# Weight k-tiles 1088 bytes apart instead of 1024, and the mixed activations at a multiple of 64 bytes

## The chip, the core and the metric

The program runs on one core of one Trainium2 chip. The metric is the device time of one execution in microseconds (us); shorter is better. The engines are TensorE (PE in the rows; PEld is its loading of weights), VectorE (DVE), ScalarE (ACT), GpSimd (POOL) and SyncE (SP, which here only issues transfers). SBUF is the on-chip memory of 128 partitions, PSUM the memory into which TensorE accumulates. All byte counts below are counts within one partition.

## The reference

One decoder block on 256 tokens of width 2048, all in float32:

```python
h = rms_norm(x, norm_mix_w)
proj = h @ w_in                       # q, k, v, z, xbc, dt, gate_a, gate_s
attn = sliding_window_attention(q, k, v, sinks, bias) @ w_attn_out
ssm = mamba2_mixer(z, xbc, dt, ...) @ w_ssm_out
mixed = sigmoid(gate_a) * attn + sigmoid(gate_s) * ssm
x = x + mixed @ w_out
u = causal_depthwise_conv(rms_norm(x, norm_ffn_w) @ w_ffn_up)
g, up = split(u, 2)
x = x + (gelu(g) * up) @ w_ffn_down
x = x + sigmoid(rms_norm(x, ple_norm_w) @ w_ple_gate) * (p @ w_ple_proj)
```

Every weight matrix is used once, so the work is a row of large products of 256 tokens with weights that come from HBM.

## The kernel before

Activations are kept with channels on partitions. A matrix of 2048 channels by 256 tokens is held as 16 k-tiles of 128 channels. To keep float32 accuracy with float32r matmuls, each activation and each weight is split in two parts, high and low: the high part is a ScalarE copy that rounds to float32r, the low part is VectorE's difference from the original. The split activations stand in tiles of `[128, k-tiles, 512]`: in each k-tile 256 columns of high parts and 256 of low parts, 2048 bytes. These tiles are `XS` (the input, for `w_in`), `YS` (for `w_ssm_out`), `AS` (for `w_attn_out`), `MS` (the mixed activations, for `w_out`), `XG` (for `w_ffn_up`, and again for `w_ple_gate`) and `FS` (for `w_ffn_down`).

Weights come in chunks of four k-tiles by 256 columns, 512 KB each. `load_chunk` (L66 to L78) issues one transfer on SP's queue into `raw` (five buffers), one ScalarE activation (L76) into `wh` and one VectorE subtraction (L77) into `wl` (three buffers each). `panel` (L95) walks over the chunks of 256 output columns and calls `products` for each k-tile:

```python
for ps, cs in zip(ps2, tiles):        # two halves of 128 output columns
    TE.matmul(ps, lhsT=wh[:, cs], rhs=x, ...)              # L84: 512 columns
for ps, cs in zip(ps2, tiles):
    TE.matmul(ps[:, 0:T], lhsT=wl[:, cs], rhs=x[:, 0:T], ...)  # L86: 256 columns
```

So one k-tile of a panel is four matmuls, called a step below: two of L84 that stream 512 columns and two of L86 that stream 256, each with a load of 128x128 weights of its own. The weights are the stationary operand, the activations the moving one. In `by_token` (L507 to L509, for q, k and v) the roles are exchanged: the stationary operand is a piece of `XS`, and the moving one a k-tile of `wh` or `wl`, 256 columns. `products_joined` (L92) is used for the very last panel.

The order of the instructions on each engine is set when the program is built. Most tiles are placed from the low end of SBUF upwards, in the order of their pools: constants, the weights' pool `wp`, small tiles, then `XS`, `YS` and the others; `MS`, `GA`, `T1` and `xt` are placed from the high end downwards.

In the built program the tiles lie as follows. Each buffer of `wh` and `wl` takes 4096 bytes and begins at a multiple of 4096, so every k-tile of weights begins at a multiple of 1024. `XS`, `YS`, `AS` and `XG` begin 64 bytes past a multiple of 2048. `FS` begins at 1472 past a multiple of 2048, which is 448 past a multiple of 512. `MS` begins at 163808, which is 480 past a multiple of 512 and 32 past a multiple of 64.

Of the kernel before, what the change touches and what calls it, by code (L numbers as in the profile page):

```python
# [10 lines left out]
F32 = mybir.dt.float32  # L11
F32R = mybir.dt.float32r
AF = mybir.ActivationFunctionType
ALU = mybir.AluOpType
# [3 lines left out]
P = 128  # L18
T = 256
D_MODEL = 2048  # L20
ND = D_MODEL // P
# [12 lines left out]
EPS = 1e-6  # L34
KC = 4
PW = 256
NEG = -1e30
RLEN = 384

# [4 lines left out]
def hybrid_block(ctx: ExitStack, tc: tile.TileContext, a: dict, out: bass.AP):  # L44
    nc = tc.nc
    V, S, G, TE = nc.vector, nc.scalar, nc.gpsimd, nc.tensor

    const = ctx.enter_context(tc.tile_pool(name="const", bufs=1))
    wp = ctx.enter_context(tc.tile_pool(name="wp", bufs=3))
# [5 lines left out]
    def acc():  # L55
        return acc_pool.tile([P, 512], F32, name="acc")

    def misc():
        return ms_pool.tile([P, 512], F32, name="ms")
# [5 lines left out]

    def load_chunk(src, kc=KC, width=PW, parts=1, before=None):  # L66
        raw = wp.tile([P, kc, width], F32, name="raw", bufs=5)
        wh = wp.tile([P, kc, width], F32R, name="wh")
        wl = wp.tile([P, kc, width], F32R, name="wl")
        n = kc // parts  # L70
        for i in range(parts):
            ks = slice(i * n, (i + 1) * n)
            if before:
                before(i)
            nc.sync.dma_start(raw[:, ks, :], src[:, ks, :])
            S.activation(wh[:, ks, :], raw[:, ks, :], AF.Copy)  # L76
            V.tensor_tensor(wl[:, ks, :], raw[:, ks, :], wh[:, ks, :].bitcast(F32), ALU.subtract)  # L77
        return wh, wl  # L78
# [32 lines left out]
    def summed(ps, name="sum", bufs=4, pool=ev):  # L111
        lo = ev.tile([P, T], F32, name="lo", bufs=4)
        S.activation(lo, ps[:, T:2 * T], AF.Copy)
        t = pool.tile([P, T], F32, name=name, bufs=bufs)
        V.tensor_tensor(t, ps[:, 0:T], lo, ALU.add)  # L115
        return t
# [10 lines left out]
    def bc(ap, shape):  # L127
        return ap.broadcast_to(shape)
# [5 lines left out]
    XS = hs_pool.tile([P, ND, 2 * T], F32R, name="XS")  # L134
# [67 lines left out]
    with tc.tile_pool(name="ssm", bufs=2) as sp:  # L202
# [28 lines left out]
        H = SSM_HEADS  # L231
# [13 lines left out]
        def step_sizes():  # L245
            raw = wp.tile([P, ND, H], F32, name="raw", bufs=5)
            nc.sync.dma_start(raw, a["w_dt"])
            psw = acc()
            for i in range(2):
                w2 = wp.tile([P, 8, 2 * H], F32R, name="wh")  # L250
                ks = slice(8 * i, 8 * i + 8)
                S.activation(w2[:, :, 0:H], raw[:, ks, :], AF.Copy)
                V.tensor_tensor(w2[:, :, H:], raw[:, ks, :], w2[:, :, 0:H].bitcast(F32), ALU.subtract)
                for k in range(8):
                    kk = 8 * i + k
                    TE.matmul(psw, lhsT=w2[:, k, :], rhs=XS[:, kk, :], start=(kk == 0), stop=(kk == ND - 1))
            scr = wp.tile([P, 8 * P], F32, name="raw", bufs=5)
            d = scr[:, 0:4 * P]
            S.activation(d, psw, AF.Copy)
            psd = misc()  # L260
            for b in range(2):
                for i in range(2):
                    TE.matmul(psd[:, b * H:(b + 1) * H], lhsT=d[:, i * T + b * P:i * T + (b + 1) * P], rhs=fold,
                              start=(i == 0), stop=(i == 1))
            dtb = scr[:, 4 * P:4 * P + H]
            nc.sync.dma_start(dtb, a["dt_bias"].partition_broadcast(P))
            ea = scr[:, 4 * P + H:5 * P]
            nc.sync.dma_start(ea, a["A_log"].partition_broadcast(P))
            S.activation(ea, ea, AF.Exp)
            xr = scr[:, 5 * P:6 * P].rearrange("p (b h) -> p b h", b=2)  # L270
            for b in range(2):
                V.scalar_tensor_tensor(xr[:, b, :], psd[:, b * H:(b + 1) * H], r_tok[:, b:b + 1], dtb,
                                       ALU.mult, ALU.add)

            e = scr[:, 6 * P:7 * P].rearrange("p (b h) -> p b h", b=2)
            V.scalar_tensor_tensor(e, xr, -1.0, xr, ALU.mult, ALU.min)
            S.activation(e, e, AF.Exp)
            z = scr[:, 7 * P:8 * P].rearrange("p (b h) -> p b h", b=2)
            V.tensor_scalar(z, e, 2.0, None, ALU.add)
            V.reciprocal(z, z)  # L280
            V.tensor_tensor(z, z, e, ALU.mult)
            z2 = scr[:, 0:P].rearrange("p (b h) -> p b h", b=2)
            V.tensor_tensor(z2, z, z, ALU.mult)
            q = scr[:, 1 * P:2 * P].rearrange("p (b h) -> p b h", b=2)
            V.tensor_scalar(q, z2, 1.0 / 17, None, ALU.mult)
            for n in (15, 13, 11, 9, 7, 5, 3):
                V.scalar_tensor_tensor(q, q, 1.0 / n, z2, ALU.add, ALU.mult)
            V.scalar_tensor_tensor(q, q, 1.0, z, ALU.add, ALU.mult)
            V.tensor_scalar(q, q, 2.0, None, ALU.mult)
            V.scalar_tensor_tensor(dt, xr, 0.0, q, ALU.max, ALU.add)  # L290
            V.scalar_tensor_tensor(dta, dt, -1.0, bc(ea.unsqueeze(1), [P, 2, H]), ALU.mult, ALU.mult)
            psa = misc()
            for c in range(2):
                TE.matmul(psa[:, c * H:(c + 1) * H], lhsT=tri, rhs=dta[:, c, :], start=True, stop=True)
            S.activation(acs, psa[:, 0:2 * H].rearrange("p (c h) -> p c h", c=2), AF.Copy)
            pah = misc()
            for c in range(2):
                TE.matmul(pah[0:H, c * P:(c + 1) * P], lhsT=dta[:, c, :], rhs=tri, start=True, stop=True)
            ach = sp.tile([H, 2 * P], F32, name="ach", bufs=1)
            S.activation(ach, pah[0:H, 0:2 * P], AF.Copy)  # L300
            nc.scalar.dma_start(acd, ach)
            pst = misc()
            TE.matmul(pst[:, 0:H], lhsT=sl32, rhs=dta[:, 0, :], start=True, stop=True)
            S.activation(dtd, pst[:, 0:H], AF.Exp)
            V.tensor_tensor(dtd, dtd, dt[:, 0, :], ALU.mult)
# [13 lines left out]
        for g in range(GROUPS):  # L319
# [60 lines left out]
            for c in range(2):  # L380
                for h in range(8):
                    j, r = h // 2, h % 2
                    TE.matmul(pys[c][r * HD:(r + 1) * HD, j * P:(j + 1) * P],  # L383
                              lhsT=xdt[:, c, h * HD:(h + 1) * HD], rhs=Es[c][:, h, :], start=True, stop=True)
# [15 lines left out]
            for pn in range(2):  # L400
                ps2 = panel(W, base, ND, XS)
                base += CH
                for i in range(2):
                    t = summed(ps2[i])
# [24 lines left out]
    for pn in range(8):  # L429
        ps2 = panel(W, base, ND, XS)  # L430
        base += CH
        for i in range(2):
            t = scaled(ps2[i], r_bc)
            S.activation(T1[:, 2 * pn + i, :], t, AF.Sigmoid)
    for pn in range(8):
        ps2 = panel(a["w_ssm_out"], pn * 2 * CH, 2 * ND, YS)
        for i in range(2):
            c = 2 * pn + i
            t = summed(ps2[i])
# [8 lines left out]
    with tc.tile_pool(name="att", bufs=2) as ap:  # L448


        tab = ap.tile([N_BUCKETS + 1, N_HEADS], F32, name="tab", bufs=1)
        V.memset(tab[N_BUCKETS:N_BUCKETS + 1, :], NEG)
        nc.sync.dma_start(tab[0:N_BUCKETS, :], a["rel_bias_table"])
# [23 lines left out]
        def normed(ps2):  # L477

            qm = ap.tile([P, 2, 4], F32, name="qm")
            for b in range(2):  # L480
                sq = ap.tile([P, 256], F32, name="ksq")
                S.activation(sq, ps2[b][:, 0:PW], AF.Square, scale=HD ** -0.5)
                V.tensor_reduce(qm[:, b, :], sq.rearrange("p (h d) -> p h d", h=4), AX.X, ALU.add)
# [3 lines left out]
            r = ap.tile([P, 2, 4], F32, name="qr")  # L487
            qn = ap.tile([P, 2, PW], F32, name="qn", bufs=3)
            for b in range(2):
                V.tensor_scalar(r[:, b, :], p[:, b, :], r_tok[:, b:b + 1], HD ** -0.5, ALU.mult, ALU.mult)  # L490
                V.tensor_tensor(qn[:, b, :].rearrange("p (h d) -> p h d", h=4),
                                ps2[b][:, 0:PW].rearrange("p (h d) -> p h d", h=4),
                                bc(r[:, b, :].unsqueeze(2), [P, 4, HD]), ALU.mult)
            return qn

        def by_token(between=None):
# [3 lines left out]
            for j in range(CH):  # L500
                wh, wl = load_chunk(W[base + j])
                for b in range(2):
                    for k in range(KC):
                        kk = j * KC + k
                        hi = XS[:, kk, b * P:(b + 1) * P]
                        lo = XS[:, kk, T + b * P:T + (b + 1) * P]
                        TE.matmul(ps2[b][:, 0:PW], lhsT=hi, rhs=wh[:, k, :], start=(kk == 0), stop=False)  # L507
                        TE.matmul(ps2[b][:, 0:PW], lhsT=hi, rhs=wl[:, k, :], start=False, stop=False)  # L508
                        TE.matmul(ps2[b][:, 0:PW], lhsT=lo, rhs=wh[:, k, :], start=False, stop=(kk == ND - 1))  # L509
# [25 lines left out]
        for g in range(N_KV):  # L535
            pk = misc()
            for b in range(2):
                for d in range(2):
                    TE.matmul(pk[d * HD:(d + 1) * HD, (1 - b) * P:(2 - b) * P],
                              lhsT=kt[:, b, g * HD:(g + 1) * HD], rhs=flip, start=True, stop=True)  # L540
# [88 lines left out]
        for kind, pn in ATT_ORDER:  # L629
# [6 lines left out]
            for i in range(2):  # L636
                t = summed(ps2[i])
# [3 lines left out]


    ms_pool2 = tc.alloc_tile_pool(name="mp2", bufs=1, side="right")
    MS = ms_pool2.tile([P, ND, 2 * T], F32R, name="MS")
    for pn in range(8):
        ps2 = panel(a["w_attn_out"], pn * CH, ND, AS)
        if pn % 4 == 0:
# [1 line left out]
        for i in range(2):  # L649
            c = 2 * pn + i  # L650
            t = summed(ps2[i])
            V.tensor_tensor(t, t, GA[:, c, :], ALU.mult)
            V.tensor_tensor(t, t, T1[:, c, :], ALU.add)
            split(MS[:, c, :], t)
    at_pool.release()
# [26 lines left out]

    residual(a["w_out"], ND, MS, g_ffn, sqa)
    ms_pool2.release()
# [33 lines left out]
    with tc.tile_pool(name="ple", bufs=2) as pp:  # L718
# [13 lines left out]
        for pn in range(8):  # L732
# [5 lines left out]
            for i in range(2):  # L738
                c = 2 * pn + i
                if pn == 7:  # L740
                    t = ev.tile([P, T], F32, name="sum", bufs=4)
                    V.tensor_tensor(t, ps2[i][:, 0:T], r3_bc, ALU.mult)
                else:
                    t = scaled(ps2[i], r3_bc)
# [107 lines left out]
```

## Time and profile before

| | |
|---|---|
| median of 3 runs | 2090.68 us (2089.81 to 2093.47) |
| profiled execution, its own time | 2089.55 us |
| its span, first to last instruction | 2087.7 us |
| mean granted TensorE clock | 0.993 |
| TensorE busy | 2046.4 us (98%) |
| VectorE busy | 1502.7 us (72%) |
| ScalarE busy | 1149.1 us (55%) |

1.9 us of the profiled execution lie outside its span. Busy times of matmuls are modelled and overlap, since matmuls are pipelined: how fast TensorE goes is read from the distance between the starts of matmuls, not from the duration of one. [...]

### The profile page before, as it was taken

What the parts mean: (1) busy time and instruction counts of PE and PEld (TensorE: products, weight loads), DVE (VectorE), ACT (ScalarE), POOL (GpSimd) and SP (SyncE); (2) the same over time, 40 slices, a digit from 0 to 9 for tenths busy, and PEclk for the clock granted to TensorE, in tenths of its full rate; (3) what the DMA queues carried; (4) which work ended last, traced back from release to release, by engine and by line L of the source; (5) the groups of instructions that cost most, each with busy time, mean ns of one, the idle gap of its engine ahead of it and who ended that gap; (6) DMA issues with size and microseconds to landing.
All of it is one profiled execution on the core that took longest, in us unless ns stands there. A gap on an engine that the chain in (4) does not pass through costs nothing.

```text
span 2087.7 us, 32510 instructions
## 1 busy us (share of the span) xinstructions
PE 2046.4 (98%) x12452; PEld 1801.5 (86%) x12452; DVE 1502.7 (72%) x2510; ACT 1149.1 (55%) x1757; POOL 181.5 (9%) x114
## 2 busy tenths in 40 slices
PE   7999999999999999999989999999999999999999
PEld 6788888888888889999868888888888888888888
DVE  7888988988755445777767667777777776555476
ACT  4667666666544444565665555555555555444454
POOL 3402222202000000101000010000000000000000
PEclk8999999999999999999999999999999999999999
DMA  5555555554455555545525655555555555555564
GB/s 191 202 183 193 181 181 178 185 183 172 172 192 192 192 192 198 181 164 170 172 95 189 230 187 191 192 192 192 191 190 189 192 189 191 192 192 188 179 208 146
DMA packets 113159, 385.49 MB, mean 185 GB/s; under 512 B 13931, under 2 KB 20972, under 8 KB 111852
## 3 DMA queue, kind: packets, MB, share of 16 engines
q1 hardware_dynamic: 103916, 366.00, 50.9%
q10 hardware_dynamic: 9088, 17.43, 2.5%
q8 instruction: 97, 1.59, 0.3%
q14 instruction: 58, 0.48, 0.1%
HBM read 381.16 MB, written 2.21 MB: 184 GB/s over the span
## 4 chain that ended last, share of the span: by engine, by line
PE 91%; DVE 4%; issue 2%; ACT 1%; POOL 1%; DMA 1%; SPq 0%; DVEq 0%; ACTq 0%; POOLq 0%
PE acc L84 53%; PE acc L86 27%; DVE wl L77 3%; PE acc L508 2%; PE acc L507 2%; PE acc L509 2%; PE ms L616 1%; PE ms L383 1%; PE acc L92 1%; ACT wh L76 0%; PE ms L607 0%; POOL zg L410 0%; POOL zg L409 0%; ACT L226 0%; PE ms L84 0%
## 5 line engine op out<-in xcount | busy, mean ns | idle before, releaser
L77 DVE TENSOR_TENSOR wl<-raw,wh 128x1024 fp32r<-128x1024 f32 (+1 forms) x700 | 888.7, 1273 | 517.9 <-ACT wh L76 515.0
L76 ACT ACTIVATE wh<-raw 128x1024 fp32r<-128x1024 f32 (+1 forms) x700 | 733.4, 1050 | 806.5 <-PE acc L84 482.9
L84 PE MATMUL acc<-XS,wh 128*128 128x512 f32 x1792 | 570.8, 398 | 9.6 <-ACT wh L76 9.5
L84 PE MATMUL acc<-XG,wh 128*128 128x512 f32 x1632 | 506.6, 392 | 0.0
L86 PEld LDWEIGHTS acc<-XS,wl 128*128 128x128 f32 x1792 | 338.0, 190 | 93.2 <-DVE wl L77 20.7
L86 PE MATMUL acc<-XS,wl 128*128 128x256 f32 x1792 | 363.3, 283 | 12.1 <-DVE wl L77 12.0
L86 PEld LDWEIGHTS acc<-XG,wl 128*128 128x128 f32 x1632 | 306.4, 188 | 67.4
L86 PE MATMUL acc<-XG,wl 128*128 128x256 f32 x1632 | 322.7, 279 | 0.0
L84 PEld LDWEIGHTS acc<-XS,wh 128*128 128x128 f32 x1792 | 276.5, 190 | 13.6 <-ACT wh L76 11.0
L84 PEld LDWEIGHTS acc<-XG,wh 128*128 128x128 f32 x1632 | 247.2, 188 | 0.0
L84 PE MATMUL acc<-FS,wh 128*128 128x512 f32 x704 | 219.6, 393 | 0.0
L84 PE MATMUL acc<-YS,wh 128*128 128x512 f32 x512 | 159.0, 392 | 0.0
L86 PEld LDWEIGHTS acc<-FS,wl 128*128 128x128 f32 x704 | 132.4, 188 | 30.0
L86 PE MATMUL acc<-FS,wl 128*128 128x256 f32 x704 | 138.9, 279 | 0.0
L680 POOL TENSOR_TENSOR sqa<-sqa,rsq 128x256 f32<-128x256 f32 x30 | 31.9, 1063 | 964.0 <-ACT rsq L679 962.9
L86 PEld LDWEIGHTS acc<-YS,wl 128*128 128x128 f32 x512 | 96.2, 188 | 21.0
L84 PEld LDWEIGHTS acc<-FS,wh 128*128 128x128 f32 x704 | 106.0, 188 | 0.0
L86 PE MATMUL acc<-YS,wl 128*128 128x256 f32 x512 | 101.0, 279 | 0.0
L508 PE MATMUL acc<-wl,XS 128*128 128x256 f32 x320 | 90.9, 284 | 0.0
L509 PE MATMUL acc<-wh,XS 128*128 128x256 f32 x320 | 90.1, 282 | 0.0
L507 PE MATMUL acc<-wh,XS 128*128 128x256 f32 x320 | 90.1, 282 | 0.0
L84 PE MATMUL acc<-AS,wh 128*128 128x512 f32 x256 | 80.9, 394 | 2.9 <-DVE sum L115 1.8
(233 smaller groups left out, 2259.4 us busy)
## 6 DMA issues: line engine op xcount, KB each, us to landing
raw<-in_w_in SPq DMA_DIRECT2D x260, 512.0 KB, 3.3
raw<-in_w_ffn_up SPq DMA_DIRECT2D x176, 512.0 KB, 3.2
raw<-in_w_ffn_down SPq DMA_DIRECT2D x88, 512.0 KB, 3.2
raw<-in_w_ssm_out SPq DMA_DIRECT2D x64, 512.0 KB, 4.2
raw<-in_w_attn_out SPq DMA_DIRECT2D x32, 512.0 KB, 3.2
raw<-in_w_out SPq DMA_DIRECT2D x32, 512.0 KB, 4.2
raw<-in_w_ple_gate SPq DMA_DIRECT2D x32, 512.0 KB, 3.3
acb<-acd ACTq DMA_DIRECT2D x8, 1024.0 KB, 4.6
```

Source lines behind the costliest of these rows:

```text
L76: S.activation(wh[:, ks, :], raw[:, ks, :], AF.Copy)
L77: V.tensor_tensor(wl[:, ks, :], raw[:, ks, :], wh[:, ks, :].bitcast(F32), ALU.subtract)
L84: TE.matmul(ps, lhsT=wh[:, cs], rhs=x, start=first, stop=False, skip_group_check=True)
L86: TE.matmul(ps[:, 0:T], lhsT=wl[:, cs], rhs=x[:, 0:T], start=False, stop=last, skip_group_check=True)
L92: TE.matmul(ps[:, 0:T], lhsT=w[:, cs], rhs=x[:, h * T:(h + 1) * T], start=first and n == 0, stop=last and n == 2)
L383: TE.matmul(pys[c][r * HD:(r + 1) * HD, j * P:(j + 1) * P], lhsT=xdt[:, c, h * HD:(h + 1) * HD], rhs=Es[c][:, h, :], start=True, stop=True)
L507: TE.matmul(ps2[b][:, 0:PW], lhsT=hi, rhs=wh[:, k, :], start=(kk == 0), stop=False)
L508: TE.matmul(ps2[b][:, 0:PW], lhsT=hi, rhs=wl[:, k, :], start=False, stop=False)
L509: TE.matmul(ps2[b][:, 0:PW], lhsT=lo, rhs=wh[:, k, :], start=False, stop=(kk == ND - 1))
L616: TE.matmul(o[h * HD:(h + 1) * HD, cs], lhsT=vt[:, b, vs], rhs=pts[:, h, ks], start=f, stop=e)
L680: G.tensor_tensor(sqa, sqa, sq, ALU.add)
```

## The change

The tiles `wh` and `wl` get 16 more float32 columns per k-tile, which nothing writes or reads. The k-tiles are then 1088 bytes apart, and a buffer takes 4352 bytes. The tile of step sizes that uses the same buffers gets 8 more columns per k-tile. `MS` gets 8 more float32 behind its last k-tile; as it is placed from the high end, its beginning moves down by 32 bytes.

```diff
+WPAD = 16
...
         raw = wp.tile([P, kc, width], F32, name="raw", bufs=5)
-        wh = wp.tile([P, kc, width], F32R, name="wh")
-        wl = wp.tile([P, kc, width], F32R, name="wl")
+        wh = wp.tile([P, kc, width + WPAD], F32R, name="wh")[:, :, 0:width]
+        wl = wp.tile([P, kc, width + WPAD], F32R, name="wl")[:, :, 0:width]
...
-                w2 = wp.tile([P, 8, 2 * H], F32R, name="wh")
+                w2 = wp.tile([P, 8, 2 * H + WPAD // 2], F32R, name="wh")
...
-                V.tensor_tensor(w2[:, :, H:], raw[:, ks, :], w2[:, :, 0:H].bitcast(F32), ALU.subtract)
+                V.tensor_tensor(w2[:, :, H:2 * H], raw[:, ks, :], w2[:, :, 0:H].bitcast(F32), ALU.subtract)
...
-                    TE.matmul(psw, lhsT=w2[:, k, :], rhs=XS[:, kk, :], start=(kk == 0), stop=(kk == ND - 1))
+                    TE.matmul(psw, lhsT=w2[:, k, 0:2 * H], rhs=XS[:, kk, :], start=(kk == 0), stop=(kk == ND - 1))
...
-    MS = ms_pool2.tile([P, ND, 2 * T], F32R, name="MS")
+    MS = ms_pool2.tile([P, ND * 2 * T + 8], F32R, name="MS")[:, 0:ND * 2 * T].rearrange("p (k t) -> p k t", k=ND)
```

The number, the order and the waits of the instructions are the same on every engine. What differs in the built program is this. The 684 whole pieces of L76 and of L77 write four runs of 256 elements with a gap of 64 bytes between them, where they wrote one run of 1024; the 16 half pieces write two runs. The six buffers begin at 0, 256 and 0 (`wh`) and at 256, 0 and 256 (`wl`) past a multiple of 512, and the k-tiles in one are 64 bytes further on each time, modulo 512. So every k-tile of weights begins at a multiple of 64, but only some at a multiple of 512. The pool `wp` is 1536 bytes larger, so `XS`, `YS`, `AS` and `XG` begin 1600 past a multiple of 2048 instead of 64, and `FS` 960 instead of 1472; modulo 512 these are 64 and 448 as before. `MS` begins at 163776, which is a multiple of 64 and 448 past a multiple of 512.

## Rows read from the trace of the kernel before

**Rows 1.** Page: busy time of each engine; granted TensorE clock in 40 slices.

```profile
PE 2046.4 (98%) x12452; PEld 1801.5 (86%) x12452; DVE 1502.7 (72%) x2510; ACT 1149.1 (55%) x1757; POOL 181.5 (9%) x114
...
PEclk8999999999999999999999999999999999999999
```

**Rows 2.** Page: the chain that ended last, by engine and by line.

```profile
PE 91%; DVE 4%; issue 2%; ACT 1%; POOL 1%; DMA 1%; SPq 0%; DVEq 0%; ACTq 0%; POOLq 0%
PE acc L84 53%; PE acc L86 27%; DVE wl L77 3%; PE acc L508 2%; PE acc L507 2%; PE acc L509 2%; PE ms L616 1%; PE ms L383 1%; PE acc L92 1%; ACT wh L76 0%; PE ms L607 0%; POOL zg L410 0%; POOL zg L409 0%; ACT L226 0%; PE ms L84 0%
```

**Rows 3.** Groups by line and shape: count, busy us, mean ns, idle before, releaser.

```profile
L84 PE MATMUL acc<-XS,wh 128*128 128x512 f32 x1792 | 570.8, 398 | 9.6 <-ACT wh L76 9.5
L84 PE MATMUL acc<-XG,wh 128*128 128x512 f32 x1632 | 506.6, 392 | 0.0
...
L84 PE MATMUL acc<-FS,wh 128*128 128x512 f32 x704 | 219.6, 393 | 0.0
L84 PE MATMUL acc<-YS,wh 128*128 128x512 f32 x512 | 159.0, 392 | 0.0
...
L84 PE MATMUL acc<-AS,wh 128*128 128x512 f32 x256 | 80.9, 394 | 2.9 <-DVE sum L115 1.8 <-DVE AS L121 0.9
L84 PE MATMUL acc<-MS,wh 128*128 128x512 f32 x256 | 80.4, 395 | 0.0
```

**Rows 4.** Windows: stretch, its us, busy us and count by engine, PEclk, DMA.

```profile
629.00:806.00 177.00, 177.00 (x1029) 155.98 (x1028) 89.20 (x97) 73.17 (x83) 0.00 (x0) 1.00 0.57 191
...
1161.00:1251.00 90.00, 90.00 (x514) 78.46 (x514) 62.35 (x82) 48.81 (x78) 14.03 (x13) 1.00 0.60 211
...
1266.00:1738.00 472.00, 472.00 (x2740) 415.60 (x2739) 361.91 (x684) 274.15 (x430) 0.00 (x0) 1.00 0.55 191
1738.00:1982.00 244.00, 244.00 (x1410) 214.01 (x1409) 132.03 (x140) 109.20 (x137) 14.05 (x13) 1.00 0.54 188
```

**Rows 5.** Timeline of PE: start us, us, instruction. First of YS, first after it.

```profile
628.89 0.62 PE L84 MATMUL acc<-YS,wh 128*128 128x512 f32 x2
...
805.54 0.28 PE L507 MATMUL acc<-wh,XS 128*128 128x256 f32 x1
```

**Rows 6.** Timeline of PE: first of FS, first after it.

```profile
1737.91 0.62 PE L84 MATMUL acc<-FS,wh 128*128 128x512 f32 x2
...
1981.97 0.40 PE L84 MATMUL acc<-XG,wh 128*128 128x512 f32 x1
```

**Rows 7.** Timeline of PE: first of MS, first after it.

```profile
1161.28 0.62 PE L84 MATMUL acc<-MS,wh 128*128 128x512 f32 x2
...
1251.21 0.39 PE L84 MATMUL acc<-XG,wh 128*128 128x512 f32 x1
```

**Rows 8.** Timeline of PE in by_token: two undisturbed stretches, first and last.

```profile
837.84 0.28 PE L507 MATMUL acc<-wh,XS 128*128 128x256 f32 x1
...
838.90 0.28 PE L507 MATMUL acc<-wh,XS 128*128 128x256 f32 x1
...
945.15 0.28 PE L507 MATMUL acc<-wh,XS 128*128 128x256 f32 x1
...
947.19 0.28 PE L507 MATMUL acc<-wh,XS 128*128 128x256 f32 x1
```

**Rows 9.** Groups by line and shape on DVE and ACT.

```profile
L77 DVE TENSOR_TENSOR wl<-raw,wh 128x1024 fp32r<-128x1024 f32 x684 | 874.8, 1282 | 517.2 <-ACT wh L76 514.2 <-PE ms L86 1.9
L76 ACT ACTIVATE wh<-raw 128x1024 fp32r<-128x1024 f32 x684 | 723.5, 1060 | 798.3 <-PE acc L84 482.0 <-issue 207.3 <-ACT fy L707 30.8
...
L395 DVE TENSOR_TENSOR ec<-ms,ec 128x512 f32<-128x512 f32 x8 | 5.4, 681 | 0.0
...
L185 ACT ACTIVATE sq<-xt 128x512 f32<-128x512 f32 x3 | 1.8, 615 | 0.0
...
L253 DVE TENSOR_TENSOR wh<-raw,wh 128x512 fp32r<-128x512 f32 x2 | 1.3, 678 | 0.0
L252 ACT ACTIVATE wh<-raw 128x512 fp32r<-128x512 f32 x2 | 1.3, 632 | 5.5 <-DVE XS L125 3.2 <-PE acc L84 2.2
```

## The prediction

> **What bounds the kernel now.** I read the page's busy times and clock first. TensorE is busy 98% of the span, VectorE 72%, ScalarE 55%, and the granted clock is full in all slices but the first [rows 1]. Then the chain of waits: 91% of the span is TensorE, 53% at L84 and 27% at L86, while the splitting on VectorE (L77) has 3% and that on ScalarE (L76) 0% [rows 2]. So the time goes with the pace at which TensorE takes one step (two matmuls of 512 columns, two of 256). There are two L84 matmuls in a step, so the counts give 896 steps on `XS`, 816 on `XG`, 352 on `FS`, 256 on `YS`, 128 on `AS` and 128 on `MS`, 2576 in all, with next to no idle time before them [rows 3].
>
> The pace cannot be read from the mean of one matmul, since matmuls overlap: 392 ns on `YS` and 395 on `MS` look alike [rows 3]. I take starts instead, in three stages in which TensorE is busy in the whole window [rows 4]. `YS`: 805.54 - 628.89 = 176.65 us for 256 steps, 0.6900 us each [rows 3, 5]. `FS`: 244.06 us for 352 steps, 0.6934 [rows 3, 6]. `MS`: 89.93 us for 128 steps, 0.7026 [rows 3, 7]. The same instructions with the same weight buffers thus have three paces, and the streamed tiles differ only in where they lie: 64, 448 and 480 bytes past a multiple of 512, the last 32 past a multiple of 64. [...]
>
> In `by_token`, where 256 columns of weights are streamed and `XS` is stationary, there are two paces in one stage: nine intervals in 1.06 us, 0.1178 each, and eighteen in 2.04, 0.1133 each [rows 8]. [...] The best pace, six times 256 columns, would make a step 0.680; this is the floor that I use.
>
> **The change, part by part.** No instruction is added, removed or moved, and no wait.
>
> *`MS` at a multiple of 64.* The stage has 128 steps. It would take the pace of `FS`, which lies at the same 448 past a multiple of 512: 128 x (0.7026 - 0.6934) = 1.2 us less. By the pace of `YS` it is 1.6, and if the 32 bytes were not the cause, 0. I take 1.2. TensorE is the bound in that stage, and VectorE is busy 62 of 90 us [rows 4], so nothing else is late next.
>
> [...]
>
> *Weight k-tiles at multiples of 64 instead of 1024.* The trace has no L84 with such weights. The nearest row is `by_token`: its stationary pieces of `XS` all lie 64 bytes past a multiple of 512, and it still reaches 0.1133 [rows 8], the best pace of all. I conclude that weights off a multiple of 512 need not cost anything, and take 0. The bounds are wide. Below: all steps at the floor, 2096 x 0.010 + 352 x 0.0134 + 128 x 0.0226 = 21.0 + 4.7 + 2.9 = 28.6 us less (`XS`, `XG`, `YS` and `AS` reckoned at the pace of `YS`). Above: all steps at the worst measured pace, that of `MS`: 2096 x 0.0126 + 352 x 0.0092 = 26.4 + 3.2 = 29.6 us more. Of `by_token`'s 960 matmuls (2% + 2% + 2% of the chain [rows 2]) a change of the fast and the slow pace by 0.0045 could make at most 4.3 us either way; I take 0.
>
> [...]
>
> *The other tiles' shift by 1536 bytes.* `XS`, `YS`, `AS`, `XG` and `FS` keep their place modulo 512. Whether a larger grid matters no row shows. I take 0; the bounds are those above.
>
> *Writing in four runs.* L77 takes 1282 ns and L76 1060. Pieces that already write runs with gaps: L253, eight runs, 678 ns against 681 for L395 of the same 512 elements in one run; L252, eight runs, 632 ns against 615 for L185 [rows 9]. So between 0 and 17 ns for a piece. What hides it: per chunk of four steps (2.76 us) VectorE needs 1.28 and ScalarE 1.06. In the fullest stage, `w_ffn_up`, VectorE is busy 362 of 472 us for 176 chunks [rows 4], so L77 could grow by 0.6 us before VectorE became the bound. Where L77 is on the chain, 3% of 2087.7 us or some 49 pieces [rows 2], 17 ns each are 0.8 us. The nearer row for VectorE is L253, so 0.
>
> *Sum.* -1.2 + 0 + 0 + 0 = -1.2 us, on the profiled 2089.55 (2087.7 of span and 1.9 around it): 2088.4. The profile lies 1.1 below the median of 2090.68, so on the median it is 2089.5.
>
> **The rivals.** A measurement of this kernel can tell about 0.2%, 4.2 us, from no change; the three runs themselves lie 3.7 apart.
>
> *Faster: the weights' place matters and spreading them helps.* For it: 0.010 to 0.0134 us of each step lies above the floor, and until now all k-tiles of weights stand at the same place modulo 512 while the streamed operand begins at a fixed distance from them; `FS` and `YS` differ in that distance, and in pace. Spread over eight distances, the stalls may get rarer. Against it: the two paces of `by_token` at the same addresses. It decides from 3.0 us over 2448 steps, 0.0012 a step. At half the way to the floor it gives 14.3 us less: 2076.4.
>
> *Slower: some of the new distances are bad ones.* The present distance on 2096 steps (64 bytes) has the best of the three paces, so a spread over eight distances can also leave it; `FS`, at 448, is 0.0034 worse. It is a mechanism of its own: TensorE stalls more in L84 and L86 while `wh` and `wl` come no later. It decides from 5.4 us over 2448 steps, 0.0022 a step. At half the way to the worst pace it gives 14.8 more: 2105.5.
>
> *The change doesn't do what it says: `MS` stays at 0.7026.* Then the 32 bytes were not the cause, and the sum is 0: 2090.7. Its time cannot be told from that of the forecast.
>
> **How the numbers follow.** Forecast 0.40, `MS` without effect 0.07, faster 0.37, slower 0.16. The first two lie within 0.2%, so faster 0.37, same 0.47, slower 0.16. The faster case reaches from 2062 to 2086, and I leave out its lower third, below 2070; the slower one from 2095 to 2120, of which I leave out what is above 2100. That is about 0.2 in all: 2070 to 2100. The forecast's own range is 2086 to 2094.
>
> **What the profile after would show.** `MS`: the first start on `MS` to the first on `XG` is 88.8 us (0.6934 a step) or 88.3 (0.690); if 89.9, that step was wrong. `YS`: 176.7 us if the place of the weights is free; 174.1 would be the floor, 179.9 the pace of `MS`. `FS`: 244.1. In `by_token` again paces of 0.113 and 0.118. L77 within 1282 to 1300 ns and L76 within 1060 to 1077, and no new idle time of TensorE before L84 or L86. The prediction is wrong if `YS` or `XG` keeps another pace than 0.690 by over 0.0015 us a step, in either direction; the sign of that decides between the rivals.

## The result and the profile after

The changed kernel takes 2122.07 us (median of four runs, 2120.32 to 2123.11) against 2092.07 for the kernel before: a ratio of 1.0147, 95% interval 1.0132 to 1.0161, so slower by 1.5%. The forecast was 2089.5, its range 2070 to 2100; the time lies above both. The profiled execution is the one of 2120.32 us, with a span of 2118.5 and a granted clock of 0.994; before it was 2089.55, 2087.7 and 0.993, so the difference to be explained is 30.8 us of span. `WPAD`'s two lines shift the numbers: L84 and L86 are now L86 and L88, L76 and L77 are L78 and L79.

The page of the changed kernel: busy times, granted clock in 40 slices, and the chain that ended last, by engine and by line.

```profile
PE 2078.9 (98%) x12452; PEld 1814.4 (86%) x12452; DVE 1509.0 (71%) x2510; ACT 1148.6 (54%) x1757; POOL 177.4 (8%) x114
...
PEclk9999999999999999999999999999999999999999
...
PE 92%; DVE 4%; ACT 2%; issue 1%; POOL 1%; DMA 0%; DVEq 0%; ACTq 0%; POOLq 0%
PE acc L86 53%; PE acc L88 27%; DVE wl L79 2%; PE acc L510 2%; PE acc L511 2%; PE acc L509 2%; PE ms L618 1%; PE ms L385 1%; POOL zg L412 1%; PE acc L94 1%; ACT wh L78 0%; POOL zg L411 0%; PE ms L609 0%; ACT L228 0%; PE ms L363 0%
```

TensorE is busy 32.5 us longer with the same 12452 instructions at the same clock, and the chain looks as it did [rows 1, 2]. No other engine has become the bound: L79 has 2% of the chain where L77 had 3%.

Groups by line and shape of the changed kernel: count, busy us, mean ns, idle before, releaser.

```profile
L79 DVE TENSOR_TENSOR wl<-raw,wh 128x1024 fp32r<-128x1024 f32 x684 | 874.3, 1281 | 540.6 <-ACT wh L78 537.1 <-PE ms L88 2.0
L78 ACT ACTIVATE wh<-raw 128x1024 fp32r<-128x1024 f32 x684 | 723.1, 1059 | 826.3 <-PE acc L86 497.1 <-issue 215.2 <-ACT fy L709 32.8
L86 PE MATMUL acc<-XS,wh 128*128 128x512 f32 x1792 | 574.2, 400 | 9.3 <-ACT wh L78 9.3
...
L86 PE MATMUL acc<-XG,wh 128*128 128x512 f32 x1632 | 514.6, 396 | 0.0
...
L86 PE MATMUL acc<-FS,wh 128*128 128x512 f32 x704 | 222.0, 396 | 0.0
```

The splits take what they took: 1281 and 1059 ns against 1282 and 1060 [rows 9]. TensorE waits no more than before: 9.3 us ahead of L86 on `XS` where it was 9.6, and 0.0 on `XG` and `FS` [rows 3]. So the time is neither in the writing with gaps nor in a wait for the weights. It is in the matmuls themselves.

The timeline of TensorE in the changed kernel: start us, us, instruction. The rows are the first on each tile, and between 1400 and 1404 us the first of each of five steps in a row.

```profile
633.62 0.63 PE L86 MATMUL acc<-YS,wh 128*128 128x512 f32 x2
...
811.96 0.28 PE L509 MATMUL acc<-wh,XS 128*128 128x256 f32 x1
...
1172.63 0.62 PE L86 MATMUL acc<-MS,wh 128*128 128x512 f32 x2
...
1261.96 0.63 PE L86 MATMUL acc<-XG,wh 128*128 128x512 f32 x2
...
1277.68 0.63 PE L86 MATMUL acc<-XG,wh 128*128 128x512 f32 x2
...
1400.92 0.63 PE L86 MATMUL acc<-XG,wh 128*128 128x512 f32 x2
...
1401.63 0.63 PE L86 MATMUL acc<-XG,wh 128*128 128x512 f32 x2
...
1402.33 0.63 PE L86 MATMUL acc<-XG,wh 128*128 128x512 f32 x2
...
1403.04 0.63 PE L86 MATMUL acc<-XG,wh 128*128 128x512 f32 x2
...
1403.75 0.63 PE L86 MATMUL acc<-XG,wh 128*128 128x512 f32 x2
...
1761.46 0.62 PE L86 MATMUL acc<-FS,wh 128*128 128x512 f32 x2
...
2010.78 0.62 PE L86 MATMUL acc<-XG,wh 128*128 128x512 f32 x2
```

The start of the 22nd step of `w_ffn_up` in the kernel before, where `XG` has 1737.91 - 1266.64 = 471.27 us for 683 steps:

```profile
1266.64 0.62 PE L84 MATMUL acc<-XG,wh 128*128 128x512 f32 x2
```

Differences of starts, divided by the steps of the stage, give the paces, beside those of before [rows 5 to 7]:

| stage | steps | before, us a step | after, us a step |
|---|---|---|---|
| `YS` | 256 | 0.6900 | 178.34 / 256 = 0.6967 |
| `MS` | 128 | 0.7026 | 89.33 / 128 = 0.6979 |
| `XG`, from the 22nd step of `w_ffn_up` on | 683 | 0.6900 | 483.78 / 683 = 0.7083 |
| `FS` | 352 | 0.6934 | 249.32 / 352 = 0.7083 |

The five single starts show that the loss is spread: intervals of 0.71, 0.70, 0.71 and 0.71 us, no one step of the four k-tiles being the long one. By stage the 30.8 us come together as 4.7 up to the start of `YS` (633.62 - 628.89), 1.7 in `YS`, 4.9 from there to `MS`, -0.6 in `MS`, 12.8 from the start of `XG` to that of `FS`, 5.3 in `FS` and 2.0 behind it. It is a loss per step, in nearly every stage.

### The profile page after: what moved, and what is told of

It reads as the page before. It is cut to its first block, busy times and chain, and to the rows that moved or that the text cites. A ratio compares the mean times of both kernels' runs of the same rounds, so it can differ in the third digit from the quotient of the medians.

```text
span 2118.5 us, 32510 instructions
## 1 busy us (share of the span) xinstructions
PE 2078.9 (98%) x12452; PEld 1814.4 (86%) x12452; DVE 1509.0 (71%) x2510; ACT 1148.6 (54%) x1757; POOL 177.4 (8%) x114
## 4 chain that ended last, share of the span: by engine, by line
PE 92%; DVE 4%; ACT 2%; issue 1%; POOL 1%; DMA 0%; DVEq 0%; ACTq 0%; POOLq 0%
PE acc L86 53%; PE acc L88 27%; DVE wl L79 2%; PE acc L510 2%; PE acc L511 2%; PE acc L509 2%; PE ms L618 1%; PE ms L385 1%; POOL zg L412 1%; PE acc L94 1%; ACT wh L78 0%; POOL zg L411 0%; PE ms L609 0%; ACT L228 0%; PE ms L363 0%
## 5 line engine op out<-in xcount | busy, mean ns | idle before, releaser
L79 DVE TENSOR_TENSOR wl<-raw,wh 128x1024 fp32r<-128x1024 f32 (+1 forms) x700 | 889.1, 1273 | 542.0 <-ACT wh L78 538.2
L78 ACT ACTIVATE wh<-raw 128x1024 fp32r<-128x1024 f32 (+1 forms) x700 | 733.1, 1049 | 834.2 <-PE acc L86 498.1
L86 PE MATMUL acc<-XS,wh 128*128 128x512 f32 x1792 | 574.2, 400 | 9.3 <-ACT wh L78 9.3
L86 PE MATMUL acc<-XG,wh 128*128 128x512 f32 x1632 | 514.6, 396 | 0.0
L88 PEld LDWEIGHTS acc<-XS,wl 128*128 128x128 f32 x1792 | 336.8, 190 | 99.4 <-DVE wl L79 22.4
L88 PE MATMUL acc<-XS,wl 128*128 128x256 f32 x1792 | 366.7, 284 | 12.0 <-DVE wl L79 11.9
L88 PEld LDWEIGHTS acc<-XG,wl 128*128 128x128 f32 x1632 | 306.0, 188 | 75.7
L88 PE MATMUL acc<-XG,wl 128*128 128x256 f32 x1632 | 328.2, 282 | 0.0
L86 PEld LDWEIGHTS acc<-XS,wh 128*128 128x128 f32 x1792 | 277.5, 190 | 13.0 <-ACT wh L78 10.9
L86 PEld LDWEIGHTS acc<-XG,wh 128*128 128x128 f32 x1632 | 250.3, 188 | 0.0
L86 PE MATMUL acc<-FS,wh 128*128 128x512 f32 x704 | 222.0, 396 | 0.0
L88 PEld LDWEIGHTS acc<-FS,wl 128*128 128x128 f32 x704 | 132.0, 188 | 32.8
L86 PE MATMUL acc<-YS,wh 128*128 128x512 f32 x512 | 159.9, 394 | 0.0
L88 PE MATMUL acc<-FS,wl 128*128 128x256 f32 x704 | 141.6, 282 | 0.0
L88 PEld LDWEIGHTS acc<-YS,wl 128*128 128x128 f32 x512 | 96.3, 188 | 22.2
L86 PEld LDWEIGHTS acc<-FS,wh 128*128 128x128 f32 x704 | 108.0, 188 | 0.0
L88 PE MATMUL acc<-YS,wl 128*128 128x256 f32 x512 | 101.5, 279 | 0.0
L86 PE MATMUL acc<-AS,wh 128*128 128x512 f32 x256 | 82.0, 398 | 3.0 <-DVE sum L117 1.8
```

The lines of the kernel that those rows point to most:

```text
L86: TE.matmul(ps, lhsT=wh[:, cs], rhs=x, start=first, stop=False, skip_group_check=True)
L88: TE.matmul(ps[:, 0:T], lhsT=wl[:, cs], rhs=x[:, 0:T], start=False, stop=last, skip_group_check=True)
```

## The experiments

**The theories.** I call *distance* the place of the streamed tile minus the place of the weights, modulo 256. Before, it is constant in a stage: 64 for `XS`, `YS`, `AS` and `XG`, 192 for `FS`, 224 for `MS`. After, the weights move on by 64 at each k-tile, so that the distance runs through 64, 0, 192 and 128 (`FS`, `MS`: 192, 128, 64, 0). The theories are: **A**, the pace goes by the distance, and the change takes most k-tiles off the good one; **B**, weights are slow off a multiple of 512 or 1024, whatever is streamed; **C**, the tiles' shift by 1536 bytes is the cause; **D**, weights written in runs with gaps are read more slowly; and later **E**, k-tiles 1088 bytes apart cost by themselves, though the distance stays. All kernels do the whole computation. Times are medians; a ratio is against the kernel before, on the same chip, with its 95% interval.

**1. `MS` alone.** Only the last line of the change is made.

```diff
-    MS = ms_pool2.tile([P, ND, 2 * T], F32R, name="MS")
+    MS = ms_pool2.tile([P, ND * 2 * T + 8], F32R, name="MS")[:, 0:ND * 2 * T].rearrange("p (k t) -> p k t", k=ND)
```

> The old k-tiles, 1024 bytes apart, in the old buffers; MS alone is moved down by 32 bytes. Theory A (the relation): TensorE's pace depends on how far the streamed tile lies from the weights modulo 256 bytes, and on whether that distance changes from k-tile to k-tile. Then every stage but MS is as before (0.690 us a step, FS 0.6934), and MS, whose distance becomes that of FS, takes 0.6934: 1.2 us less in all. Theory B (weights must begin at a multiple of 512 or 1024): the same. Theory C (the tiles that moved by 1536 bytes cost the time): the same, as nothing else moves here. Theory D (writing in four runs with gaps slows ScalarE and VectorE or disturbs TensorE): the same. If MS stays at 0.7026, its 32 bytes were not the cause.

Measured: 2089.3 us, ratio 0.9994 (0.9984 to 1.0003). The timeline of TensorE in this kernel, first on `MS` and first after it:

```profile
1163.48 0.62 PE L84 MATMUL acc<-MS,wh 128*128 128x512 f32 x2
...
1252.24 0.63 PE L84 MATMUL acc<-XG,wh 128*128 128x512 f32 x2
```

88.76 us for 128 steps is 0.6934, the pace of `FS`, which has the same distance of 192. Moving `MS` by 32 bytes is worth 1.2 us, as forecast, and the loss lies in the weights' part. All kernels below move `MS` by these 32 bytes too, or further.

**2. The buffers' size alone.** They take 4352 bytes, so all tiles shift by 1536 as in the change, but a buffer's k-tiles stand 1024 apart, in one run.

```diff
-        wh = wp.tile([P, kc, width], F32R, name="wh")
+        wh = wp.tile([P, n + 64], F32R, name="wh")[:, 0:n].rearrange("p (k w) -> p k w", k=kc)   # n = kc * width; wl alike
```

> The buffers are as large as in the changed kernel (4352 bytes, so they begin at multiples of 256 and all other tiles move by 1536 bytes), MS is moved, but the k-tiles stand 1024 bytes apart and are written in one run. Theory A: the distance modulo 256 is the same for all k-tiles, so 0.690 us a step as before and about 2091 us. Theory B: five of the six buffers now begin off a multiple of 1024 and three off one of 512, so most steps take 0.697 to 0.708 as in the changed kernel, 2110 to 2120 us. Theory C: all moved tiles cost as in the changed kernel, 2122 us. Theory D: one run, so as before, 2091 us.

Measured: 2090.06 us, ratio 0.9999 (0.9990 to 1.0009). The timeline of TensorE, first on `YS` and first after it:

```profile
628.34 0.39 PE L85 MATMUL acc<-YS,wh 128*128 128x512 f32 x1
...
804.98 0.28 PE L508 MATMUL acc<-wh,XS 128*128 128x256 f32 x1
```

176.64 us, 0.6900 a step: nothing has changed. C falls. The buffers begin at 0 and 256 past a multiple of 512 here, so B falls for beginnings off 512 as well, and a distance that differs by 256 made no difference, 0.6900 in `YS` either way: this is why distances are taken modulo 256.

**3. Written in four runs, but 2048 bytes apart.** `wh` and `wl` share a buffer and alternate in it, so each piece writes four runs of 256 elements with gaps, and every k-tile still begins at a multiple of 1024.

```diff
-        wh = wp.tile([P, kc, width], F32R, name="wh")
-        wl = wp.tile([P, kc, width], F32R, name="wl")
+        both = wp.tile([P, kc, 2, width], F32R, name="wh")
+        wh, wl = both[:, :, 0, :], both[:, :, 1, :]
```

> High and low weights share a buffer, k-tile by k-tile, so that the k-tiles of each are 2048 bytes apart; all begin at multiples of 1024, no other tile moves, MS is moved. L76 and L77 write four runs with gaps of 1024 bytes. Theory A: one distance for all, 0.690 us a step and about 2091 us. Theory B and C: as before, 2091 us. Theory D: the gaps stand in the changed kernel too, so 2122 us here.

Measured: 2078.91 us, ratio 0.9951 (0.9936 to 0.9965). The timeline of TensorE, first on `YS` and first after it:

```profile
622.61 0.39 PE L84 MATMUL acc<-YS,wh 128*128 128x512 f32 x1
...
799.25 0.28 PE L507 MATMUL acc<-wh,XS 128*128 128x256 f32 x1
```

Again 176.64 us, 0.6900 a step, so D falls. That this kernel is faster than the kernel before I had not expected. It is not the pace. Windows of the first experiment's kernel, two stretches (us, busy us and count of PE, PEld, DVE, ACT and POOL, granted clock, DMA share, GB/s):

```profile
60.00:610.00 550.00, 536.11 (x3269) 466.92 (x3269) 463.37 (x716) 341.88 (x455) 111.28 (x56) 0.99 0.53 182
1090.00:1160.00 70.00, 67.23 (x387) 58.65 (x386) 47.39 (x80) 34.84 (x53) 0.00 (x0) 0.98 0.50 171
```

And the same windows of this one:

```profile
60.00:610.00 550.00, 539.13 (x3308) 470.33 (x3307) 461.00 (x718) 331.22 (x448) 109.21 (x56) 0.99 0.54 185
1090.00:1160.00 70.00, 70.00 (x408) 61.54 (x407) 49.77 (x81) 35.01 (x52) 0.00 (x0) 1.00 0.62 217
```

TensorE is idle 10.9 us in the first stretch instead of 13.9, and not at all in the second instead of 2.8, in which it also gets through 21 matmuls more. A shared buffer has other dependencies, and the order set at building comes out differently. The first `YS` step starts at 622.61 instead of 628.89 [rows 5] and the first `MS` step at 1151.42 instead of 1161.28 [rows 7]. Which step of that order makes the gain I did not follow up.

**4. All weights 64 bytes on.** As the second, but the weights begin 64 bytes into their buffers. The distance is constant again, 0 for `XS`, `YS`, `AS` and `XG`, and 128 for `FS` and `MS`.

```diff
-        wh = wp.tile([P, kc, width], F32R, name="wh")
+        wh = wp.tile([P, n + 64], F32R, name="wh")[:, 16:16 + n].rearrange("p (k w) -> p k w", k=kc)   # wl alike
```

> As in the run with larger buffers and k-tiles 1024 bytes apart, but all weights begin 64 bytes further on. The distance is then 0 modulo 256 for XS, YS, AS and XG, and 128 for FS and MS, the same for all k-tiles. Theory A: the distance does not change within a stage, so the pace is near 0.690 or better (the smallest group of YS in the changed kernel, at distance 0, sums to 0.687): 2070 to 2095 us. Theory B: no k-tile at a multiple of 512 any more, 2120 us or worse. Theory C: 2122 us. Theory D: 2091 us.

Measured: 2106.47 us, ratio 1.0083 (1.0068 to 1.0098). The timeline of TensorE, first on `YS` and on `FS`, and first after each:

```profile
631.74 0.40 PE L85 MATMUL acc<-YS,wh 128*128 128x512 f32 x1
...
810.09 0.28 PE L508 MATMUL acc<-wh,XS 128*128 128x256 f32 x1
...
1750.99 0.63 PE L85 MATMUL acc<-FS,wh 128*128 128x512 f32 x2
...
1996.25 0.61 PE L85 MATMUL acc<-XG,wh 128*128 128x512 f32 x2
```

178.35 us for 256 steps and 245.25 for 352 are both 0.6967. Nothing but a constant shift of the weights by 64 bytes costs 0.8% of the whole. The pace that I expected, near 0.690, fell; the place of the weights counts even where it never changes.

**5. Streamed tiles spaced like the weights.** The change with `XS`, `YS`, `AS`, `XG`, `FS` and `MS` also 64 bytes wider per k-tile, so that both operands move together and the distance stays 64 or 192. For room `raw` has four buffers here instead of five, so that paces are compared and not whole times.

```diff
-    YS = y_pool.tile([P, 4 * GROUPS, 2 * T], F32R, name="YS")
+    YS = y_pool.tile([P, 4 * GROUPS, 2 * T + WPAD], F32R, name="YS")[:, :, 0:2 * T]   # the others alike
```

> The changed kernel, but the streamed tiles move with the weights: their k-tiles stand 2112 bytes apart instead of 2048, so that streamed tile and weights keep one distance modulo 256 (64 for XS, YS, AS, XG; 192 for FS and MS), while the weights stand 1088 apart. To make room raw has four buffers instead of five, so only the pace of a step is to be compared, not the whole time. Theory A (the relation): 0.690 us a step in YS and XG, 0.6934 in FS and MS, as before. Rival E (weights that move from k-tile to k-tile cost by themselves, whatever the streamed tile does): 0.697 to 0.708 as in the changed kernel.

Measured: 2109.4 us (two runs). The timeline of TensorE, first on `YS` and on `FS`, and first after each:

```profile
634.26 0.39 PE L86 MATMUL acc<-YS,wh 128*128 128x512 f32 x1
...
812.18 0.28 PE L509 MATMUL acc<-wh,XS 128*128 128x256 f32 x1
...
1755.90 0.39 PE L86 MATMUL acc<-FS,wh 128*128 128x512 f32 x1
...
2002.88 0.39 PE L86 MATMUL acc<-XG,wh 128*128 128x512 f32 x1
```

`YS` has 177.92 / 256 = 0.6950 and `FS` 246.98 / 352 = 0.7016; `XG` has 0.6984. These lie between before and after. A in its simple form, that a constant distance keeps the pace, falls; E is right in part. Either moving costs something by itself, or the distance that counts isn't quite constant: loads and matmuls overlap (PEld is busy 86% of the span beside PE's 98% [rows 1]), so the weights of a matmul may be loaded while the matmul ahead still streams, and at each new k-tile that one would read 64 bytes short of the constant distance. The second is argued, not shown.

**6. Two places, 128 bytes apart.** A gap of 128 behind each second k-tile; the distances go 64, 64, 192, 192.

```diff
-        wh = wp.tile([P, kc, width], F32R, name="wh")
+        wh = wp.tile([P, kc // 2, 2 * width + 32], F32R, name="wh")[:, :, 0:2 * width]   # wl alike; L76 and L77 write two runs of 512
```

> A gap of 128 bytes behind the second k-tile of a chunk, none behind the others: two k-tiles at distance 64 modulo 256 and two at 192 (XS, YS, AS, XG; the other way round for FS and MS), two changes of distance per chunk instead of four. If a step's pace is only that of its own distance, it is the mean of 0.6900 and 0.6934, 0.6917 in all stages, 2092 to 2095 us. If each change of distance costs besides, as the 0.697 to 0.708 of the changed kernel suggest (the mean of the four constant paces is 0.6942), the pace is 0.694 to 0.700 and the time 2100 to 2115 us.

Measured: 2091.82 us, ratio 1.0006 (0.9997 to 1.0016). The timeline of TensorE, as above:

```profile
630.98 0.39 PE L95 MATMUL acc<-YS,wh 128*128 128x512 f32 x1
...
808.04 0.28 PE L518 MATMUL acc<-wh,XS 128*128 128x256 f32 x1
...
1743.78 0.39 PE L95 MATMUL acc<-FS,wh 128*128 128x512 f32 x1
...
1987.27 0.40 PE L95 MATMUL acc<-XG,wh 128*128 128x512 f32 x1
```

177.06 / 256 = 0.6916 and 243.49 / 352 = 0.6917: `YS` is slower than before and `FS` faster, and both come to the mean of 0.6900 and 0.6934. So the paces of the two distances simply mix, this change by 128 costs nothing, and the numbers are as if the same distance gave the same pace at another place of the weights, which speaks for A and against B.

**7. All stages at distance 64.** The third kernel, with `MS` moved by 160 bytes instead of 32, and `FS` by 128 with a wider table ahead of it.

```diff
+    MS = ms_pool2.tile([P, ND * 2 * T + 40], F32R, name="MS")[:, 0:ND * 2 * T].rearrange("p (k t) -> p k t", k=ND)
...
+        fw = fp.tile([P, 2 * NF * 3 + 32], F32, name="fw", bufs=1)[:, 0:2 * NF * 3].rearrange("p (c k) -> p c k", k=3)
```

> The run with shared buffers (2078.9 us) with FS and MS moved so that they too lie at distance 64 modulo 256 from the weights. Theory A: both stages take 0.6900 instead of 0.6934, (352 + 128) x 0.0034 = 1.6 us less: 2077.3 us. If FS and MS are slower for another reason than their distance (their place as such, or what else runs in those stages), they keep 0.6934 and the time is 2078.9.

Measured: 2077.62 us, ratio 0.9931 (0.9915 to 0.9948). The timeline of TensorE, first on `MS` and on `FS`, and first after each:

```profile
1152.72 0.39 PE L84 MATMUL acc<-MS,wh 128*128 128x512 f32 x1
...
1241.04 0.39 PE L84 MATMUL acc<-XG,wh 128*128 128x512 f32 x1
...
1727.74 0.39 PE L84 MATMUL acc<-FS,wh 128*128 128x512 f32 x1
...
1970.62 0.39 PE L84 MATMUL acc<-XG,wh 128*128 128x512 f32 x1
```

88.32 / 128 and 242.88 / 352 are both 0.6900, where they were 0.7026 and 0.6934 [rows 6, 7]. A moved tile takes the pace of its new distance. This version beats both kernels.

**8. All weights 32 bytes on.** As the fourth with `[:, 8:8 + n]`: distances 32 and 160.

> As the run with all weights 64 bytes on, but 32: the weights, and not the streamed tile, lie off the grid of 64. Theory A in its plain form (only the distance counts, in steps of 64): distance 32 lies between 0 (0.6967) and 64 (0.6900), so 0.690 to 0.697 us a step. Rival F (any operand off the grid of 64 costs as MS did): about 0.7026 a step, 2115 to 2120 us.

Measured: 2104.56 us, ratio 1.0061 (1.0041 to 1.0081). `YS` takes 808.74 - 631.25 = 177.49 us, 0.6933 a step, `FS` 1996.38 - 1748.81 = 247.57, 0.7033. `XS`, at the same constant distance as `YS`, is not always as fast: 13 steps from 157.18 us on take 9.18 us, 0.706.

**9. Two places, 64 bytes apart.** As the sixth with a gap of 64: the distances go 64, 64, 0, 0 (`FS`: 192, 192, 128, 128).

```diff
+        wh = wp.tile([P, kc * width + 64], F32R, name="wh")[:, 0:kc // 2 * (2 * width + 16)]   # in two parts of 2 * width + 16; wl alike
```

> As the run with a gap of 128 bytes behind the second k-tile, but 64: distances 64, 64, 0, 0 modulo 256 in a chunk (XS, YS, AS, XG) and 192, 192, 128, 128 (FS, MS). If a step's pace is only that of its distance when it stands still, the means are (0.6900 + 0.6967) / 2 = 0.6934 and (0.6934 + 0.6967) / 2 = 0.6950, and the time is 2098 to 2101 us. If a change of distance by 64 costs besides, as the 0.695 and 0.7016 with both tiles moving suggest, there are two such changes per chunk instead of the changed kernel's four: 0.695 to 0.701, 2102 to 2112 us.

Measured: 2112.97 us, ratio 1.0103 (1.0088 to 1.0118). The timeline of TensorE, first on `YS` and on `MS`, and first after each:

```profile
634.01 0.40 PE L95 MATMUL acc<-YS,wh 128*128 128x512 f32 x1
...
813.21 0.28 PE L518 MATMUL acc<-wh,XS 128*128 128x256 f32 x1
...
1174.13 0.39 PE L95 MATMUL acc<-MS,wh 128*128 128x512 f32 x1
...
1263.41 0.40 PE L95 MATMUL acc<-XG,wh 128*128 128x512 f32 x1
```

The means of the constant distances would be (0.6900 + 0.6967) / 2 = 0.6934 for `YS` and (0.6934 + 0.6967) / 2 = 0.6950 for `FS`. Measured are 179.20 / 256 = 0.7000 and, for `FS`, (2004.67 - 1757.10) / 352 = 247.57 / 352 = 0.7033, longer by 6.6 and 8.3 ns a step. Here, unlike in the sixth, the mixture does not explain it: where the distance changes by 64, something is added. It is not a fixed price for each change, though: `MS`, with the distances of `FS`, has 89.28 / 128 = 0.6975, only 2.5 ns above the mean.

**10 and 11. Distances 96 and 80 throughout.** The seventh with `wh` and `wl` 224 or 240 bytes into their shared buffer.

```diff
+        both = wp.tile([P, n + 64], F32R, name="wh")[:, 56:56 + n].rearrange("p (k h w) -> p k h w", k=kc, h=2)   # n = kc * 2 * width; 60 in the eleventh
```

> The run with everything at distance 64, but the weights 32 bytes lower: distance 96 in all stages. The paces at distances 0, 32 and 64 were 0.6967, 0.6934 and 0.6900, a line; if it goes on, 0.6867, and the time is 2577 x 0.0033 = 8.5 us below 2077.6. If it turns towards the 0.6967 of distance 128, 0.693, 7.7 us above. If weights off the grid of 64 cost as they did at distance 160, 0.703, 34 us above.

> The same at distance 80, 16 bytes lower instead of 32. On the line, 0.6884, 4.1 us below 2077.6; if 64 is the lowest point, 0.6917, 4.4 us above; if an operand off a grid of 32 or 64 costs by itself, 0.70 or more.

Measured: 2106.72 us, ratio 1.0075 (1.0060 to 1.0090), and 2103.18, ratio 1.0057 (1.0041 to 1.0074). The timeline of TensorE in the tenth, first on `YS` and first after it:

```profile
629.42 0.39 PE L85 MATMUL acc<-YS,wh 128*128 128x512 f32 x1
...
808.62 0.28 PE L508 MATMUL acc<-wh,XS 128*128 128x256 f32 x1
```

179.20 us, 0.7000 a step, in both kernels, though in the tenth `MS` has (1257.44 - 1166.98) / 128 = 0.7067, and `FS` (1997.61 - 1751.21) / 352 = 0.7000 again. Their distance is the same and constant, so even then it does not settle the pace alone. The pace in `YS` falls from distance 0 over 32 to 64, but it doesn't go on falling: 64 is the best that was tried. Sixteen bytes away from it a step costs 0.010 us more in `YS`, and in `FS` and `MS` as well (246.40 / 352 and 89.60 / 128).

**12. The changed kernel again,** for a second trace.

> The changed kernel once more, for a second trace. In its first trace YS (0.6967) and XG (0.708) had different paces at the same distances 64, 0, 192, 128. If the program settles which of the two a stage gets, the same stages have the same paces again; if it is settled by chance at the beginning of a stage, some stage changes sides, and the whole time with it (XG alone by some 9 us).

Measured: 2120.87 us (one run). The timeline of TensorE, the same stretch of `XG` as above:

```profile
1278.23 0.39 PE L86 MATMUL acc<-XG,wh 128*128 128x512 f32 x1
...
1762.01 0.39 PE L86 MATMUL acc<-FS,wh 128*128 128x512 f32 x1
```

Again 483.78 us, 0.7083 a step, and in `YS` again 0.6967; these stages kept their paces. In `XS` it is otherwise. The timeline of TensorE in the first trace, first and end of 40 steps in a row on `XS`:

```profile
183.20 0.62 PE L86 MATMUL acc<-XS,wh 128*128 128x512 f32 x2
...
211.06 0.59 PE L350 MATMUL ms<-BC 128*128 128x256 f32 x2
```

And the same 40 steps in the second trace:

```profile
182.80 0.63 PE L86 MATMUL acc<-XS,wh 128*128 128x512 f32 x2
...
211.13 0.59 PE L350 MATMUL ms<-BC 128*128 128x256 f32 x2
```

27.86 us are 0.6965 a step, 28.33 are 0.7083: the same instructions on the same tiles, in one program, at either pace. Within the first trace, too, 24 steps on `XS` take 16.99 us (539.73 to 556.72), 0.7079 each, and a few steps later 102 take 71.07 (562.55 to 633.62), 0.6968. `MS` goes from one pace to the other: its first 16 steps take 11.31 us (1172.63 to 1183.94), 0.7069, and its mean is 0.6979. So with the changed weights there are two paces at the same four distances. What decides which of them a stretch takes was not tested.

## Why the prediction was wrong

**The step that failed is "Weight k-tiles at multiples of 64 instead of 1024", taken at 0.** I took its price from the two paces of `by_token`, whose stationary pieces lie off a multiple of 512 [rows 8]. But all of them lie 64 past a multiple of 256 while all its streamed weights lie at 0, so its distance is one and the same. A row with one constant distance can't price a change that makes the distance vary. The fourth experiment shows that the weights' place counts even alone.

What the runs put in its place is two terms. First the mixture: the four distances have 0.6900, 0.6967, 0.6934 and 0.6967, a mean of 0.6942. Over 2096 steps from 0.6900, 352 from 0.6934 and 128 from 0.7026 that is 8.8 + 0.3 - 1.1 = 8.0 us. Second, the other 30.8 - 8.0 = 22.8 us, which the mixture does not give: with the distance changing by 64 from step to step a stretch goes at 0.6967 or at 0.7083, both above 0.6942. `YS`, most of `MS` and a part of `XS` have the first, 2.5 ns above the mean; `XG`, `FS` and the rest of `XS` have the second, 14 ns above it (the twelfth experiment). As an estimate from these paces, all steps at the first would have lost 14.4 us and all at the second 44.3; the measured 30.8 lie between. That the weights' changing places bring the loss is shown, since the first three experiments leave nothing else of the change that touches these stages; why there are two paces is not. In `by_token`, also taken at 0, the fast stretches are gone: 52 intervals in a row take 6.14 us (834.77 to 840.91), 0.118 each, where they took 5.90 (828.25 to 834.15), 0.113, and from its first matmul to its last it takes 177.6 us instead of 175.4. These 2.2 us are a part of the 22.8.

**The rival was right, its size was not.** "Slower: some of the new distances are bad ones" named the loss and its mark, more time in L84 and L86 while `wh` and `wl` come no later: `XG` went from 0.6900 to 0.7083 a step with 0.0 us of idle time before its wide matmuls. It counted eight distances, modulo 512; by the second experiment only four of them differ. Its price, half the way to the worst pace, was 14.8 us. The upper bound of the term taken at 0, all steps at the worst measured pace, was 29.6 more, and the measured loss lies just beyond it. That the two come so close is chance, since the bound was a pace of `MS` and the loss is a mixture of others: `XG` and `FS` came to 0.7083, a pace that no stage of before had. At the chance of 0.16 I cut it at 2100 and so left out what happened. The argument against "Faster", that the two paces of `by_token` come at the same addresses, was read rightly: its distance is one throughout, and two paces at the same places are what `XS` shows in the changed kernel. But it speaks neither for nor against "Faster", which is refuted by the time.

**What was right.** `MS` took the pace of `FS` when it alone was moved (0.6934; -1.2 us, the first experiment). In the changed kernel it got 0.6979, where its weights move as well. The other tiles' shift cost nothing (the second). Writing in four runs cost nothing per piece, 1281 and 1059 ns. And the mark set for the prediction's failure, `YS` or `XG` off 0.690 by over 0.0015, is what the trace shows, by 0.0067 and 0.0183.

**What stays open.** What holds up the matmuls, which no run here shows. Why a change by 64 costs and the one by 128 that was tried does not. Why steps with the same distances go at 0.6967 or at 0.7083, and what settles which. Whether the fifth kernel is slower by the moving itself or by a load that overlaps the step ahead. And whether the distance alone counts: for 64 and 192 the sixth experiment tried a second place of the weights, but each of the other distances was held constant at one pair of places only, and 32, 80, 96 and 160 only with weights off a multiple of 64.

## What to carry to other kernels

Where TensorE is the bound, look at the byte places of both matmul operands modulo 256, not at each one's own alignment: read the pace of a stage from starts of matmuls, shift one operand by 32 or 64 bytes, and keep the distance that is best constant over all k-tiles and stages (here 64, with 0.6900 us a step, where the worst constant one had 0.7067). Padding that moves each k-tile on by 64 bytes modulo 256 was what cost the time here, 30.8 us of span. Measure more than one stretch and more than one execution, since steps at the same places can have two paces, here 0.6967 and 0.7083. And a row can price a new layout only if in that row the thing varies that the change lets vary.

## What the runs showed of the hardware that was not expected

With weights and streamed operand at a constant distance, a step of 1536 columns had these paces, in executions whose mean granted clock was 0.992 to 0.995:

| distance, bytes modulo 256 | us a step | where |
|---|---|---|
| 0 | 0.6967 | `YS`, fourth |
| 32 | 0.6933, 0.706 | `YS`, a part of `XS`, eighth |
| 64 | 0.6900 | `YS` before; `MS`, `FS`, seventh |
| 80 | 0.7000 | `YS`, `FS`, `MS`, eleventh |
| 96 | 0.7000, 0.7067 | `YS`, `MS`, tenth |
| 128 | 0.6967 | `FS`, fourth |
| 160 | 0.7033 | `FS`, eighth |
| 192 | 0.6934 | `FS` before; `MS`, first |
| 224 | 0.7026 | `MS` before |

Between the best and the worst of these lie 2.4% of a step. With the distance moving by 64 at each step 0.6967 and 0.7083 were seen, the latter 2.7% above the best, on the same tile in one execution and on the same 40 steps in two. On `XG` and `FS` the profile has no idle time ahead of the wide matmuls: the loss shows in the distance between starts.
